# Splitting five heads' outputs at the store instead of at the load, in layer 1 of a two-layer decoder trunk

## The chip, the cores and the metric

The kernel runs on one core of a Trainium2 chip. Its time is the device time of one execution in microseconds (us); the time before is the median of three runs, 1315.35 us (1311.99 to 1317.4). The engines are named as in the profile: PE (TensorE; PEld is its weight loading), DVE (VectorE), ACT (ScalarE), POOL (GpSimd) and SP (SyncE, which here issues nearly all transfers). TensorE's granted clock is given as a share of full speed; 1.00 and 0.50 are its two levels, 2.4 and 1.2 GHz.

## The reference

The input x is one sequence of 1024 positions by 1024 features in fp32. Layer 0 is a differential attention with 6 heads, layer 1 a stick-breaking attention with 12 heads of 64 features on keys and values computed once after layer 0. Both layers also attend to 256 memory tokens with 4 heads, multiply all outputs by a SiLU gate, and end in an output projection whose result is added to the residual. What concerns us is the end of layer 1:

```python
z = einsum(q, k) * scale;  log_beta = log_sigmoid(z)
log_1m = where(mask, log_sigmoid(-z), 0)
suffix = cumsum(log_1m, reverse=True) - log_1m
a = exp(where(mask, log_beta + suffix, -inf));  o = einsum(a, v)
y = concatenate([o, memory_attention]) * silu(gate)      # 1024 x 1024
out = x1 + y @ b_w_out
```

Everything is fp32.

## The kernel before, in words

Every matrix product is made of fp32r operands split in two parts, a "hi" part (a cast to fp32r) and a "lo" part (the value minus that cast). `mm3` (L402) issues three matmuls: hi by hi, hi by lo, lo by hi. So each operand costs a cast and a subtract before PE can use it.

The columns of y are in 8 tiles of 128: tiles 0 to 5 are the heads of layer 1 (each tile holds two of the reference's 12 heads; "head" means such a pair from here on, counted from 0), tiles 6 and 7 are the memory attention. The positions are in two halves c of 512, each of two quarters of 256.

Layer 1 runs in slots (`run_layer`, from n = 0): the memory units take the first 8, and head h takes slots 8 + 8h to 8 + 8h + 8, with its last sums in the slot after. In a slot PE makes scores (`sc`), ACT turns them to sigmoids `u` and `be` (L936, L937), POOL masks `be` (L941), DVE scans `u` (L943) and multiplies `be` by it: that is the weight matrix of one block. One slot later PE transposes it (`tw`, L517; ACT casts it to `wT`, L521, and DVE subtracts), and PE multiplies it with the values (`av`, L965); ACT copies half of that to `avt` (L975), DVE adds it to `y`, POOL multiplies `y` by the gate. The PSUM tiles `tw` and `av` share a pool of three banks, so that a new `tw` may have to wait until DVE's `y` has read an older `av`. `T_`, `ws`, `sc`, `avs` in `run_layer` are these steps' instruction lists, and `merge` interleaves them with the slot's fill work (projections, loads of weights) by cost. This hand-written order is the order of PE's instructions; a scheduler orders those of the other engines, and every engine and queue then works strictly in its own order.

Where does y go? For the last head (h = 5) it goes to `split_y` (L568): ACT casts it into the hi part of `yh`, POOL subtracts for the lo part, both at once in SBUF. The other five heads and the memory tiles go to `store_y` (L543): SP writes the fp32 `y` to `y_dr` in DRAM, since `yh` (pool `hp`, two buffers) takes the place of the hidden state `h`, which is in use until then. `out_proj` (L1005) later loads a tile back (`load`, L1009): a transfer to `ys`, an ACT cast (L1014) and a DVE subtract (L1015), giving `yh` hi and lo. Fourteen such loads are made, seven for each c. Which slot a load goes to is written in `tail` (L1335): B = 48 is the first slot of head 5, `load0` and `load1` are the loads for c = 0 and 1 in the tile order 0, 1, 2, 3, 4, 6, 7, and `go0`, `go1` the products `po` of the output projection.

`ys`, the output weights `w` (raw weights in `raw`, cast at L124, subtract on POOL through the helper at L94), the residual `res` and the memory's `hm` are in one pool, `wp`, with 11 buffers. `L94` is the line of a helper for all tensor-by-tensor operations, so that the tile names tell them apart.

Of the kernel before, what the change touches and what calls it, by code (L numbers as in the profile page):

```python
# [8 lines left out]
F32 = mybir.dt.float32  # L9
F32R = mybir.dt.float32r  # L10
BF16 = mybir.dt.bfloat16
AF = mybir.ActivationFunctionType
ALU = mybir.AluOpType
# [7 lines left out]
NH = 6  # L21
# [18 lines left out]
def trunk(ctx: ExitStack, tc: tile.TileContext, xT, memT, pos, gains, vecs, wA, wAm, wAg, wAo,  # L40
          wB, wBm, wBg, wBo, wM, invf, out):
    nc = tc.nc
    P = 128
# [16 lines left out]
    ppj = ctx.enter_context(tc.tile_pool(name="ppj", bufs=2, space=PSUM))  # L60
    ptr = ctx.enter_context(tc.tile_pool(name="ptr", bufs=3, space=PSUM))

    y_dr = [drp.tile([2, 8, P, 512], F32, name=f"y_dr{l}") for l in range(2)]
    v_dr = [[drp.tile([P, 4, 256], F32, name=f"v_dr{h}{c}") for c in range(2)] for h in range(NH)]
    x1_dr = drp.tile([2, P, 8, 512], F32, name="x1_dr")

# [26 lines left out]
    def tt(eng, out_, a, b, op):  # L93
        eng.tensor_tensor(out_, a, b, op)  # L94
# [303 lines left out]
    def merge(main, fill):  # L398
        for _, f in mixed(main, fill):
            f()  # L400
# [140 lines left out]
        return [(109 * min(4, b + 1 - 4 * g), lambda g=g: go(g)) for g in range((b + 4) // 4)]  # L541

    def store_y(l, t, c, y):  # L543
        nc.sync.dma_start(y_dr[l][c // 2, t, :, (c % 2) * 256:(c % 2) * 256 + 256], y)

    splits = {}

    def y_split(l, c):

        if (l, c) not in splits:  # L550
            splits[(l, c)] = hp.tile([P, 2, 8, 512], F32R, name="yh", tag="h")
        return splits[(l, c)]
# [334 lines left out]
    class StickUnit:  # L887
# [62 lines left out]
        def W(self, bc):  # L950
            b, c = bc
            cc = b // 2
            r = causal_wT(self, b, bc)
            if b % 2 == 0:
                return r, [], []

            def av(part, k0, k1):
                if c == 0 and k0 == 0 and part == 0:
                    self.avt = wk.tile([P, 256], F32, name="avt", tag="tmp")
                if k0 == 0 and part == 0:  # L960
                    self.avp = ptr.tile([P, 512], F32, name="av", tag="tr")
                o = self.avp[:, :256]
                for kb in range(k0, k1):
                    v = self.v[kb // 4][:, kb % 4, 2 * c:2 * c + 2, :]
                    T.matmul(o, v, self.wT[kb // 4][:, part, kb % 4, :], start=(part == 0 and kb == 0),  # L965
                             stop=(part == 1 and kb == b))
                if part == 0 or k1 <= b:
                    return
                if c == 0:
                    self.y = wk.tile([P, 256], F32, name="y", tag="y")  # L970
                tmp = self.avt
                lo, hi = (slice(0, 64), slice(64, 128))
                d, s_ = (lo, hi) if c == 0 else (hi, lo)
                with urgent():
                    S.copy(tmp[d, :], o[s_, :])  # L975
                    tt(V, self.y[d, :], o[d, :], tmp[d, :], ALU.add)
                if c == 1:
                    tt(G, self.y, self.y, silu_cols(1, self.h, cc), ALU.mult)
                    (split_y if self.h == NH - 1 else store_y)(1, self.h, cc, self.y)
            return r, [(218, lambda p=p, k=k: av(p, k, k + 2)) for p in range(2) for k in range(0, b + 1, 2)], []  # L980

    def value_chunks(p, ws, b):
# [22 lines left out]
    def out_proj(l, c, wo):  # L1005
        st = {}
        x1_st[c] = st

        def load(t):  # L1009
            yh = y_split(l, c)  # L1010
            if l == 1:
                ys = wp.tile([P, 512], F32, name="ys", tag="w")
                nc.sync.dma_start(ys, y_dr[l][c, t])
                S.copy(yh[:, 0, t, :], ys)  # L1014
                tt(V, yh[:, 1, t, :], ys, yh[:, 0, t, :].bitcast(F32), ALU.subtract)  # L1015
                return
            ys = vp.tile([P, 2, 512], F32, name="ys", tag="v")
            nc.sync.dma_start(ys, y_dr[l][c, t:t + 2].rearrange("t p n -> p t n"))
            for j in range(2):
                G.tensor_scalar(yh[:, 0, t + j, :], ys[:, j, :], 1.0, 0.0, ALU.mult, ALU.add)  # L1020
                tt(G, yh[:, 1, t + j, :], ys[:, j, :], yh[:, 0, t + j, :].bitcast(F32), ALU.subtract)


        order = tuple(range(8)) if l == 0 else (0, 1, 2, 3, 4, 6, 7, 5)

        def go(m, i):
            if i == 0:
                st["f", m] = load_packed(wo[m], way="act" if m < 2 or (l == 1 and c == 0) else "vector")
                st["ps", m] = ppj.tile([P, 512], F32, name="po", tag="pj")
                if l == 1:  # L1030
                    st["res", m] = wp.tile([P, 512], F32, name="res", tag="w")
                    nc.sync.dma_start(st["res", m], x1_dr[c][:, m, :])
                elif m % 2 == 0:
                    st["res"] = vp.tile([P, 2, 512], F32, name="res", tag="v")
                    nc.sync.dma_start(st["res"], xT[c][:, m:m + 2, :])
            f, yh, ps = st["f", m], y_split(l, c), st["ps", m]
            t = order[i]
            mm3(ps, (f(0, t), f(1, t)), (yh[:, 0, t, :], yh[:, 1, t, :]), i == 0, i == 7)
            if i == 7:
                res = st["res"][:, m % 2, :] if l == 0 else st["res", m]  # L1040
                tt(V, res, ps, res, ALU.add)
                if l == 0:
                    if m == 0:
                        st["a"] = kp.tile([P, 2, 512], F32, name="accs", tag="k")
                    with urgent(HP if m == 7 else 0):
                        squares(st["a"], res, m)
                    if m % 2:
                        nc.sync.dma_start(x1_dr[c, :, m - 1:m + 1, :], st["res"])
                else:
                    nc.sync.dma_start(out[c, m], res)  # L1050
        def without(m, i):

            if i == 0:
                st["f", m] = load_packed(wo[m], way="act")
                st["ps", m] = ppj.tile([P, 512], F32, name="po", tag="pj")
                st["res", m] = wp.tile([P, 512], F32, name="res", tag="w")
                nc.sync.dma_start(st["res", m], x1_dr[c][:, m, :])
            f, yh, ps, t = st["f", m], y_split(l, c), st["ps", m], order[i]
            mm3(ps, (f(0, t), f(1, t)), (yh[:, 0, t, :], yh[:, 1, t, :]), i == 0, i == 6)
            if i == 6:  # L1060
                tt(V, st["res", m], ps, st["res", m], ALU.add)
                if m == EARLY - 1:
                    st["w5"] = load_w(wo[0:EARLY, :, order[7], :].rearrange("m p n -> p m n"), EARLY * P, way="act")

        def last(m):
            yh, w, t = y_split(l, c), st["w5"], order[7]
            ps = ppj.tile([P, 512], F32, name="po", tag="pj")
            o = slice(m * P, (m + 1) * P)
            mm3(ps, (w[:, 0, o], w[:, 1, o]), (yh[:, 0, t, :], yh[:, 1, t, :]), True, True)
            tt(V, st["res", m], ps, st["res", m], ALU.add)  # L1070
            nc.sync.dma_start(out[c, m], st["res", m])
        items = [[(C512, lambda m=m, i=i: go(m, i)) for i in range(8)] for m in range(8)]
        if l == 1 and c == 0:
            items[:EARLY] = [[(C512, lambda m=m, i=i: without(m, i)) for i in range(7)] for m in range(EARLY)]
            items[EARLY + 1:EARLY + 1] = [[(C512, lambda m=m: last(m)) for m in range(EARLY)]]
        return ([(0, lambda t=t: load(t)) for t in ((0, 2, 4) if l == 0 else order[:7])],
                [x for m in items for x in m])

# [193 lines left out]
    def run_layer(l, mem, planned, early, tail):  # L1272
# [4 lines left out]
        for n in range(min(fills), max(ss) + lag + (2 if l == 0 else 1)):  # L1277
# [11 lines left out]
            if l == 0:  # L1289
                sc = flat(sc)  # L1290
                ws, avs = flat(ws), flat(avs)
                if n >= 48:
                    main += fins[:1] + ws + sc[:2] + avs + fins[1:] + sc[2:] + T_
                else:
                    main += fins[:1] + ws + T_ + sc[:2] + avs + fins[1:] + sc[2:]
            else:
                if n > 8:
                    slack = [[(1500, lambda: None)]] if avs else []
                    order = [T_] + ws[:1] + sc[:1] + ws[1:2] + sc[1:2] + slack + avs + sc[2:] + ws[2:]
                else:  # L1300
                    order = ws + sc + [T_] + avs
                main += flat(order)
# [11 lines left out]
    def ends(l, wo):  # L1314
# [17 lines left out]
    load0, go0 = out_proj(1, 0, wBo)  # L1332
    load1, go1 = out_proj(1, 1, wBo)
    B = 8 * NH
    tail = {B + 1: load0[:2], B + 2: load0[2:4] + go0[:4], B + 3: load0[4:] + go0[4:10], B + 4: go0[10:16],  # L1335
            B + 5: go0[16:21], B + 6: go0[21:29], B + 7: go0[29:39], B + 8: go0[39:49] + load1[:2], B + 9: go0[49:55] + load1[2:5]}
    run_layer(1, mems[1], (fills, ts, ss), {}, tail)
    merge([], load1[5:] + go0[55:] + go1)


def _layout(inputs):
# [64 lines left out]
```

## Time and profile before

| | |
|---|---|
| median of three runs | 1315.35 us |
| profiled execution | 1313.52 us |
| its span, first to last instruction | 1311.7 us |
| mean granted clock | 0.98 |
| PE busy | 1241.6 us, 95% of the span |
| PE weight loading | 1107.8 us, 84% |
| DVE busy | 963.2 us, 73% |
| ACT busy | 851.2 us, 65% |
| POOL busy | 729.4 us, 56% |
| chain that ended last | PE 71%, DVE 11%, ACT 5%, DMA 5%, issue 4%, POOL 4% |

The times of the rows below are counted from the first instruction of the span. The shares are averages over the whole span; layer 1's heads run from about 800 us on, head 4 begins near 1082, head 5 near 1155, and the last matmul of the output projection ends near 1308. A wait is the idle time of an engine in front of one instruction, with the instruction that released it. A busy PE at half the clock counts as busy as one at full clock, so stalls and clock have to be read apart.

### The profile page before, as it was taken

How to read it: one execution, taken by the hardware profiler on the slowest of the kernel's cores; microseconds unless marked ns; L12 is line 12 of the kernel's file. 1: busy time of each engine (PE TensorE's matmuls, PEld its weight loads, DVE VectorE, ACT ScalarE, POOL GpSimd, SP SyncE). 2: the span in 40 equal slices, each digit the busy share in tenths (PEclk: the TensorE clock that was granted, in tenths of full speed). 3: DMA queues.
4: the chain of work that ended last, by engine and by line, in shares of the span. 5: the costliest groups of instructions: out<-in, count | busy, mean ns of one | idle time of the engine just before them, and what ended most of it. 6: DMA issues, size and time to landing. Idle time of an engine off the chain costs nothing.

```text
span 1311.7 us, 22804 instructions
## 1 busy us (share of the span) xinstructions
PE 1241.6 (95%) x7396; PEld 1107.8 (84%) x7396; DVE 963.2 (73%) x2129; ACT 851.2 (65%) x2295; POOL 729.4 (56%) x943
## 2 busy tenths in 40 slices
PE   7799999999999899999989999999999999989898
PEld 6699999999999889877868897889788987878777
DVE  8887777788787875864946545897878787788932
ACT  4676667566676766863657866676767676666621
POOL 7664545445353567946046855765666566557620
PEclk9899999999999999999999999999999999989989
DMA  6010101101020222256550142112121222222453
GB/s 220 25 51 27 55 23 43 39 11 60 21 65 21 81 67 77 86 179 222 174 171 25 43 134 61 50 53 92 55 69 35 99 69 64 63 78 91 152 163 114
DMA packets 76071, 105.85 MB, mean 81 GB/s; under 512 B 8368, under 2 KB 60720, under 8 KB 75696
## 3 DMA queue, kind: packets, MB, share of 16 engines
q1 hardware_dynamic: 75664, 104.24, 25.1%
q8 instruction: 59, 0.97, 0.3%
q14 instruction: 60, 0.49, 0.1%
q10 hardware_dynamic: 288, 0.15, 0.0%
HBM read 82.87 MB, written 21.50 MB: 80 GB/s over the span
## 4 chain that ended last, share of the span: by engine, by line
PE 71%; DVE 11%; ACT 5%; DMA 5%; issue 4%; POOL 4%; SPq 0%; DVEq 0%; POOLq 0%; ACTq 0%
PE pq L404 6%; PE pq L406 6%; PE pq L405 6%; PE tw L517 5%; PE pg L404 4%; PE pg L405 4%; PE pg L406 4%; PE sc L506 4%; PE sc L507 3%; PE av L965 3%; PE po L405 2%; PE po L404 2%; PE po L406 2%; PE pv L404 2%; PE pk L404 2%
## 5 line engine op out<-in xcount | busy, mean ns | idle before, releaser
L94 POOL TENSOR_TENSOR w<-raw,w 128x384 fp32r<-128x384 f32 (+1 forms) x183 | 207.0, 1140 | 37.9 <-ACT w L124 30.0
L943 DVE TENSOR_TENSOR_SCAN u<-u,stick 128x128 f32<-128x128 f32 (+3 forms) x96 | 145.2, 1512 | 27.1 <-ACT u L936 26.8
L404 PE MATMUL pq<-w,h 128*128 128x384 f32 (+1 forms) x448 | 159.3, 356 | 6.1 <-ACT h L224 5.5
L94 DVE TENSOR_TENSOR wT<-tw,wT 128x512 fp32r<-128x512 f32 (+2 forms) x248 | 138.6, 565 | 26.0 <-ACT wT L521 24.1
L406 PE MATMUL pq<-w,h 128*128 128x384 f32 (+1 forms) x448 | 148.7, 332 | 3.0 <-DVE h L225 2.9
L405 PE MATMUL pq<-w,h 128*128 128x384 f32 (+1 forms) x448 | 148.3, 331 | 0.8 <-POOL w L94 0.7
L521 ACT CAST wT<-tw 128x512 fp32r<-128x512 f32 (+2 forms) x248 | 121.9, 497 | 33.8 <-PE tw L517 30.7
L941 POOL TENSOR_SCALAR_AFFINE_SELECT be<-be 128x128 f32<-128x128 f32 x96 | 82.2, 857 | 84.8 <-ACT be L937 84.6
L124 ACT CAST w<-raw 128x384 fp32r<-128x384 f32 (+1 forms) x145 | 67.7, 486 | 69.0 <-PE po L406 42.9
L101 POOL TENSOR_TENSOR ss<-ss,mhalf 128x4 f32<-128x4 f32 x68 | 71.2, 1049 | 73.0 <-DVE ss L352 72.3
L404 PE MATMUL pg<-h,w 128*128 128x512 f32 x256 | 109.2, 427 | 0.0
L811 ACT ACTIVATE e<-sc,nmd 128x512 f32<-128x512 f32 (+2 forms) x144 | 82.6, 579 | 36.1 <-DVE nmd L808 33.6
L404 PE MATMUL po<-yh,w 128*128 128x512 f32 x256 | 104.7, 409 | 1.0 <-DVE res L94 0.7
L405 PE MATMUL po<-yh,w 128*128 128x512 f32 x256 | 101.5, 397 | 2.4 <-POOL yh L94 2.4
L405 PE MATMUL pg<-h,w 128*128 128x512 f32 x256 | 103.2, 403 | 0.0
L406 PE MATMUL pg<-h,w 128*128 128x512 f32 x256 | 103.2, 403 | 0.0
L406 PE MATMUL po<-yh,w 128*128 128x512 f32 x256 | 101.3, 396 | 0.0
L517 PE MATMUL tw<-identR,be 128*128 128x128 f32 x432 | 74.7, 284 | 23.0 <-DVE y L94 20.4
L94 DVE TENSOR_TENSOR be<-be,u 128x127 f32<-128x127 f32 (+3 forms) x96 | 83.9, 875 | 14.2 <-POOL be L941 10.3
L404 PEld LDWEIGHTS pq<-w,h 128*128 128x128 f32 x448 | 85.2, 190 | 9.0 <-POOL w L122 5.5
L405 PEld LDWEIGHTS pq<-w,h 128*128 128x128 f32 x448 | 85.4, 191 | 4.0 <-POOL w L94 1.5
L406 PEld LDWEIGHTS pq<-w,h 128*128 128x128 f32 x448 | 84.9, 189 | 4.0 <-DVE h L225 4.0
(239 smaller groups left out, 3914.5 us busy)
## 6 DMA issues: line engine op xcount, KB each, us to landing
raw<-in_wA_dram SPq DMA_DIRECT2D x44, 192.0 KB, 2.4
raw<-in_wBo_dram SPq DMA_DIRECT2D x33, 192.0 KB, 2.5
raw<-in_wAo_dram SPq DMA_DIRECT2D x32, 192.0 KB, 2.8
v_dr<-vs SPq DMA_DIRECT2D x48, 128.0 KB, 1.8
v<-v_dr SPq DMA_DIRECT2D x12, 512.0 KB, 3.4
raw<-in_wB_dram SPq DMA_DIRECT2D x36, 128.0 KB, 2.2
raw<-in_wB_dram SPq DMA_DIRECT2D x24, 192.0 KB, 2.4
wkv<-in_wM_dram SPq DMA_DIRECT2D x16, 256.0 KB, 3.3
```

The costliest lines, as they stand in the source:

```text
L94: eng.tensor_tensor(out_, a, b, op)
L101: G.tensor_tensor(t, t, mhalf[:, :n], ALU.pow)
L124: S.copy(w[:, 0, :n], raw[:, :n])
L404: T.matmul(o, a[0], b[0], start=first, stop=False)
L405: T.matmul(o, a[0], b[1], start=False, stop=False)
L406: T.matmul(o, a[1], b[0], start=False, stop=last)
L506: T.matmul(sc[:, :m], qh, k[:, c, :m], start=True, stop=False)
L517: T.transpose(t[:, j * P:(j + 1) * P], w[:, j * P:(j + 1) * P], identF)
L521: S.copy(hi, t3)
L811: S.activation(e[:, o:o + n], st["sc"][j], AF.Exp, bias=nm[:, 0:1], scale=-1.0 if j == len(ps) - 1 else 1.0, accum_out=st["l"][:, j, c:c + 1])
L941: G.affine_select(out=be[:, L - P:L], in_=be[:, L - P:L], pattern=[[-1, P]], compare_op=ALU.is_gt, fill=0.0, base=0, channel_multiplier=1)
L943: V.tensor_tensor_scan(u[:, 0:L][:, ::-1], u[:, 0:L][:, ::-1], keep["m"][:, 1024 - L:1024][:, ::-1], 1.0, ALU.mult, ALU.max)
```

## The change

`y_dr` gets one more dimension of 2 (hi and lo). For heads 0 to 4 `store_y` is replaced by `store_split`: it only puts a function on the list `late`. `flush`, a step of its own in every slot above 8 behind the first scores, takes what is on the list. In the slot after the sums it makes the split (ACT copies `y` to `ysp` hi, 128x256, POOL subtracts for lo; the buffer is one of `wp`) and puts the store on the list; one slot later it issues the store, 256 KB instead of 128 KB. `load` for tiles 0 to 4 of layer 1 is now one transfer of 512 KB from `y_dr` straight into `yh`, with no cast and no subtract; tiles 6 and 7 are loaded as before. The lists in `tail` move: tiles 6 and 7 of c = 0 to slot B + 2, tile 4 to B + 3, the five of c = 1 from B + 8 and B + 9 to B + 6, and those of tiles 6 and 7 of c = 1 behind two more products at the end.

In numbers: ten of the fourteen casts (128x512, ACT) and ten of the fourteen subtracts (128x512, DVE) go. Twenty ACT copies and twenty POOL subtracts of 128x256 come. Twenty stores and ten loads double in size. PE's instructions and their order are the same.

```diff
--- before.py
+++ after.py
@@ -60,7 +60,7 @@
     ppj = ctx.enter_context(tc.tile_pool(name="ppj", bufs=2, space=PSUM))
     ptr = ctx.enter_context(tc.tile_pool(name="ptr", bufs=3, space=PSUM))
 
-    y_dr = [drp.tile([2, 8, P, 512], F32, name=f"y_dr{l}") for l in range(2)]
+    y_dr = [drp.tile([2, 8, 2, P, 512], F32, name=f"y_dr{l}") for l in range(2)]
     v_dr = [[drp.tile([P, 4, 256], F32, name=f"v_dr{h}{c}") for c in range(2)] for h in range(NH)]
     x1_dr = drp.tile([2, P, 8, 512], F32, name="x1_dr")
 
@@ -541,7 +541,23 @@
         return [(109 * min(4, b + 1 - 4 * g), lambda g=g: go(g)) for g in range((b + 4) // 4)]
 
     def store_y(l, t, c, y):
-        nc.sync.dma_start(y_dr[l][c // 2, t, :, (c % 2) * 256:(c % 2) * 256 + 256], y)
+        nc.sync.dma_start(y_dr[l][c // 2, t, 0, :, (c % 2) * 256:(c % 2) * 256 + 256], y)
+
+    late = []
+
+    def store_split(l, t, c, y):
+
+        def split():
+            s = wp.tile([P, 2, 256], F32R, name="ysp", tag="w")
+            S.copy(s[:, 0, :], y)
+            tt(G, s[:, 1, :], y, s[:, 0, :].bitcast(F32), ALU.subtract)
+            late.append(lambda: nc.sync.dma_start(
+                y_dr[l][c // 2, t, :, :, (c % 2) * 256:(c % 2) * 256 + 256].rearrange("s p n -> p s n"), s.bitcast(F32)))
+        late.append(split)
+
+    def flush():
+        for f in [late.pop(0) for _ in range(len(late))]:
+            f()
 
     splits = {}
 
@@ -976,7 +992,7 @@
                     tt(V, self.y[d, :], o[d, :], tmp[d, :], ALU.add)
                 if c == 1:
                     tt(G, self.y, self.y, silu_cols(1, self.h, cc), ALU.mult)
-                    (split_y if self.h == NH - 1 else store_y)(1, self.h, cc, self.y)
+                    (split_y if self.h == NH - 1 else store_split)(1, self.h, cc, self.y)
             return r, [(218, lambda p=p, k=k: av(p, k, k + 2)) for p in range(2) for k in range(0, b + 1, 2)], []
 
     def value_chunks(p, ws, b):
@@ -1008,14 +1024,17 @@
 
         def load(t):
             yh = y_split(l, c)
+            if l == 1 and t < NH:
+                nc.sync.dma_start(yh[:, :, t, :].bitcast(F32), y_dr[l][c, t].rearrange("s p n -> p s n"))
+                return
             if l == 1:
                 ys = wp.tile([P, 512], F32, name="ys", tag="w")
-                nc.sync.dma_start(ys, y_dr[l][c, t])
+                nc.sync.dma_start(ys, y_dr[l][c, t, 0])
                 S.copy(yh[:, 0, t, :], ys)
                 tt(V, yh[:, 1, t, :], ys, yh[:, 0, t, :].bitcast(F32), ALU.subtract)
                 return
             ys = vp.tile([P, 2, 512], F32, name="ys", tag="v")
-            nc.sync.dma_start(ys, y_dr[l][c, t:t + 2].rearrange("t p n -> p t n"))
+            nc.sync.dma_start(ys, y_dr[l][c, t:t + 2, 0].rearrange("t p n -> p t n"))
             for j in range(2):
                 G.tensor_scalar(yh[:, 0, t + j, :], ys[:, j, :], 1.0, 0.0, ALU.mult, ALU.add)
                 tt(G, yh[:, 1, t + j, :], ys[:, j, :], yh[:, 0, t + j, :].bitcast(F32), ALU.subtract)
@@ -1296,7 +1315,7 @@
             else:
                 if n > 8:
                     slack = [[(1500, lambda: None)]] if avs else []
-                    order = [T_] + ws[:1] + sc[:1] + ws[1:2] + sc[1:2] + slack + avs + sc[2:] + ws[2:]
+                    order = [T_] + ws[:1] + sc[:1] + [[(0, flush)]] + ws[1:2] + sc[1:2] + slack + avs + sc[2:] + ws[2:]
                 else:
                     order = ws + sc + [T_] + avs
                 main += flat(order)
@@ -1332,10 +1351,10 @@
     load0, go0 = out_proj(1, 0, wBo)
     load1, go1 = out_proj(1, 1, wBo)
     B = 8 * NH
-    tail = {B + 1: load0[:2], B + 2: load0[2:4] + go0[:4], B + 3: load0[4:] + go0[4:10], B + 4: go0[10:16],
-            B + 5: go0[16:21], B + 6: go0[21:29], B + 7: go0[29:39], B + 8: go0[39:49] + load1[:2], B + 9: go0[49:55] + load1[2:5]}
+    tail = {B + 1: load0[:4], B + 2: go0[:2] + load0[5:6] + go0[2:4] + load0[6:], B + 3: load0[4:5] + go0[4:10], B + 4: go0[10:16],
+            B + 5: go0[16:21], B + 6: load1[:5] + go0[21:29], B + 7: go0[29:39], B + 8: go0[39:49], B + 9: go0[49:55]}
     run_layer(1, mems[1], (fills, ts, ss), {}, tail)
-    merge([], load1[5:] + go0[55:] + go1)
+    merge([], go0[55:57] + load1[5:] + go0[57:] + go1)
 
 
 def _layout(inputs):
```

At the start of head 5 DVE has this order in the kernel before, from the cast keys `k` of head 5 to the `y` of head 4 that frees the bank for the next transposes (`u<-u,stick` is the scan, `tw` and `wT` the transposed weights):

```order
L94 TENSOR_TENSOR k<-pk,k 64x512 x2
L94 TENSOR_TENSOR yh<-ys,yh 128x512 x4
L94 TENSOR_TENSOR wT<-tw,wT 128x3x128
L943 SCALAR_TENSOR_TENSOR u<-u,stick 128x896
...
L943 SCALAR_TENSOR_TENSOR u<-u,stick 128x1024
L94 TENSOR_TENSOR yh<-ys,yh 128x512
L94 TENSOR_TENSOR be<-be,u 128x1023
L94 TENSOR_TENSOR yh<-ys,yh 128x512
L94 TENSOR_TENSOR ql<-pq,qh 64x512 x2
L94 TENSOR_TENSOR yh<-ys,yh 128x512
L94 TENSOR_TENSOR y<-av,avt 64x256
```

The same place in the kernel after (its lines are 16 higher):

```order
L94 TENSOR_TENSOR k<-pk,k 64x512 x2
L94 TENSOR_TENSOR wT<-tw,wT 128x3x128
L959 SCALAR_TENSOR_TENSOR u<-u,stick 128x896
L94 TENSOR_TENSOR wT<-tw,wT 128x4x128
L94 TENSOR_TENSOR be<-be,u 128x895
L94 TENSOR_TENSOR wT<-tw,wT 128x4x128
L959 SCALAR_TENSOR_TENSOR u<-u,stick 128x1024
L94 TENSOR_TENSOR be<-be,u 128x1023
L94 TENSOR_TENSOR ql<-pq,qh 64x512 x2
L94 TENSOR_TENSOR y<-av,avt 64x256
```

The seven subtracts of `yh` that stood between `k` and `y` are gone from the place.

At the start of head 4 ACT has this order in the kernel before, from the `avt` of head 3 through the two pieces of sigmoids of a block of seven tiles (L152 casts turned weights):

```order
L975 COPY avt<-av 64x256
L521 CAST wT<-tw 128x4x128
L914 CAST k<-pk 64x512 x2
L521 CAST wT<-tw 128x3x128
L936 ACTIVATE u<-sc 128x512
L937 ACTIVATE be<-sc 128x512
L936 ACTIVATE u<-sc 128x384
L937 ACTIVATE be<-sc 128x384
```

And in the kernel after:

```order
L991 COPY avt<-av 64x256
L521 CAST wT<-tw 128x4x128
L930 CAST k<-pk 64x512 x2
L521 CAST wT<-tw 128x3x128
L552 CAST ysp<-y 128x256
L152 ACTIVATE w<-raw,gn 128x128 x3
L952 ACTIVATE u<-sc 128x512
L953 ACTIVATE be<-sc 128x512
L952 ACTIVATE u<-sc 128x384
L953 ACTIVATE be<-sc 128x384
```

The copy of the `y` of head 3 has come between `wT` and the sigmoids, and with it three casts of weights that stood behind them.

In the last slot DVE has this order before, from a scan to the last head's `y`:

```order
L943 SCALAR_TENSOR_TENSOR u<-u,stick 128x1024
L94 TENSOR_TENSOR yh<-ys,yh 128x512
L94 TENSOR_TENSOR res<-po,res 128x512
L94 TENSOR_TENSOR yh<-ys,yh 128x512
L94 TENSOR_TENSOR be<-be,u 128x1023
L94 TENSOR_TENSOR yh<-ys,yh 128x512
L94 TENSOR_TENSOR y<-av,avt 64x256
```

And after:

```order
L959 SCALAR_TENSOR_TENSOR u<-u,stick 128x1024
L94 TENSOR_TENSOR be<-be,u 128x1023
L94 TENSOR_TENSOR res<-po,res 128x512
L94 TENSOR_TENSOR yh<-ys,yh 128x512 x2
L94 TENSOR_TENSOR y<-av,avt 64x256
```

Only the subtracts of tiles 6 and 7 are left, and both stand directly ahead of `y`.

## Rows read from the trace of the kernel before

**Rows 1.** The page, part 1: busy us, share of the span, instructions.
```profile
PE 1241.6 (95%) x7396; PEld 1107.8 (84%) x7396; DVE 963.2 (73%) x2129; ACT 851.2 (65%) x2295; POOL 729.4 (56%) x943
```

**Rows 2.** Waits of PE, then SP's queue: line, releaser: us in total, times, longest.
```profile
PE tw L517 <- DVE y L94: 20.4, 7, 6.8
...
SPq L544 <- POOL y L94: 100.0, 22, 15.1
```

**Rows 3.** PE's timeline: start us, us, instruction, [idle before <-releaser].
```profile
675.30 1.02 PE L233 MATMUL ms<-onesD,accs 128*128 128x1 f32 x8 [2.13 <-DVE accs L94]
...
947.09 0.66 PE L517 MATMUL tw<-identR,be 128*128 128x128 f32 x4 [2.86 <-DVE y L94]
...
1094.85 1.11 PE L517 MATMUL tw<-identR,be 128*128 128x128 f32 x4 [2.90 <-DVE y L94]
...
1172.89 1.11 PE L517 MATMUL tw<-identR,be 128*128 128x128 f32 x4 [5.71 <-DVE y L94]
...
1248.99 1.11 PE L517 MATMUL tw<-identR,be 128*128 128x128 f32 x4 [6.85 <-DVE y L94]
```

**Rows 4.** Stretches: engines' busy us (instructions), granted clock, DMA share, GB/s.
```profile
675.00:679.00 4.00, 3.70 (x31) 3.73 (x32) 0.95 (x5) 1.36 (x4) 4.00 (x5) 1.00 0.60 211
...
1170.00:1176.00 6.00, 3.11 (x12) 2.71 (x13) 5.14 (x10) 1.50 (x3) 1.92 (x4) 0.50 0.45 130
...
1245.00:1255.00 10.00, 6.01 (x19) 5.04 (x20) 6.38 (x8) 2.88 (x6) 4.71 (x5) 0.50 0.61 184
1260.00:1300.00 40.00, 40.00 (x179) 33.10 (x178) 12.99 (x25) 9.38 (x20) 2.27 (x3) 1.00 0.55 172
```

**Rows 5.** DVE's timeline, start of head 5: one y to the next.
```profile
1154.14 0.43 DVE L94 TENSOR_TENSOR y<-av,avt 64x256 f32<-64x256 f32 x1
...
1172.42 0.42 DVE L94 TENSOR_TENSOR y<-av,avt 64x256 f32<-64x256 f32 x1
```

**Rows 6.** DVE's groups of instructions, 1154 to 1173: busy us, mean ns, idle before.
```profile
L94 DVE TENSOR_TENSOR yh<-ys,yh 128x512 fp32r<-128x512 f32 x7 | 5.7, 849 | 0.1
```

**Rows 7.** Tile yh, from 1100 on: ns min/median/max, first and last start.
```profile
L404 PE MATMUL po<-yh,w x128: 389/389/775, 1182.6 to 1307.0; 128*128 128x512 f32 x128
...
L1014 ACT CAST yh<-ys x14: 614/622/717, 1155.6 to 1241.4; 128x512 fp32r<-128x512 f32 x14
L94 DVE TENSOR_TENSOR yh<-ys,yh x14: 676/710/1479, 1157.0 to 1247.1; 128x512 fp32r<-128x512 f32 x14
L571 ACT CAST yh<-y x4: 403/406/410, 1195.0 to 1259.9; 128x256 fp32r<-128x256 f32 x4
L94 POOL TENSOR_TENSOR yh<-y,yh x4: 738/841/1062, 1196.6 to 1260.8; 128x256 fp32r<-128x256 f32 x4
```

**Rows 8.** ACT's timeline, head 4's last sums.
```profile
1179.92 0.36 ACT L975 COPY avt<-av 64x256 f32<-64x256 f32 x1 [2.60 <-PE av L965]
```

**Rows 9.** Timelines of ACT, POOL and DVE at the start of head 4.
```profile
1080.79 0.60 ACT L936 ACTIVATE u<-sc 128x512 f32<-128x512 f32 x1
...
1086.31 0.99 ACT L152 ACTIVATE w<-raw,gn 128x128 fp32r<-128x128 f32 x3 [0.18 <-PE pq L406]
...
1081.55 0.73 POOL L94 TENSOR_TENSOR y<-y,sl 128x256 f32<-128x256 f32 x1 [3.42 <-DVE y L94]
...
1089.09 2.87 POOL L94 TENSOR_TENSOR w<-raw,w 128x384 fp32r<-128x384 f32 x1
...
1084.11 2.16 DVE L943 TENSOR_TENSOR_SCAN u<-u,stick 128x896 f32<-128x896 f32 x1
...
1088.37 2.79 DVE L943 TENSOR_TENSOR_SCAN u<-u,stick 128x1024 f32<-128x1024 f32 x1
```

**Rows 10.** DVE's timeline in the last slot.
```profile
1240.52 2.28 DVE L943 TENSOR_TENSOR_SCAN u<-u,stick 128x1024 f32<-128x1024 f32 x1
...
1248.52 0.41 DVE L94 TENSOR_TENSOR y<-av,avt 64x256 f32<-64x256 f32 x1
```

**Rows 11.** Tile ys: from issue to landing.
```profile
DMA to landing us min/median/max: 2.5/3.1/4.8
```

## The prediction

> **What bounds the kernel now.** I read the page's busy shares first, then the waits of TensorE, then where on TensorE's timeline those waits lie, and last what the releasing engine did before each. PE is busy for 1241.6 of 1311.7 us [rows 1]: whatever leaves PE's own order alone can win only PE's idle time, and time in which PE runs below full clock. The change leaves PE's instructions and their order as they are. Of PE's waits in layer 1 one kind is large, the transpose of new weights into tw, released by VectorE's y: 20.4 us in 7 waits [rows 2]. Four of them make 18.3 us: 2.86 and 2.90 at the starts of heads 2 and 4 (counted from 0), 5.71 at the start of head 5 and 6.85 in the last slot [rows 3]. I call the last two A and B. tw doesn't read y; it takes the PSUM bank that y is last to read.
>
> The clock is the second price. After A it stands at 0.50 in 1170 to 1176, after B in 1245 to 1255 [rows 4], the lower of its two levels. PE resumed at 1172.89 and ran about 3.5 us at half rate, so lost 1.75; after B it resumed at 1248.99 and ran 5.9 us so (to about 1255), and lost 3.0. A pause of 2.13 us at 675.30 left the clock at 1.00 [rows 3, 4]; after the 2.90 one at 1094.85 four transposes took 1.11 us, as after A and B, at the half rate [rows 3]. So the price of the clock falls away only where a pause is cut to about 2 us. From 1260 to 1300 PE is busy for 40.00 of 40.00 us at 1.00 [rows 4]: nothing can be won there.
>
> **A: the start of head 5.** VectorE goes from one y at 1154.14 to the next at 1172.42 with hardly a gap [rows 5], and seven subtracts yh<-ys,yh take 5.7 us of that [rows 6]. The new order has none of them there; five of the ten removed ones belong to this place, and the other two go later, with their tiles. y would then start near 1166.8 and end near 1167.2. PE is ready at 1172.89 - 5.71 = 1167.18 and needs a moment after y. I take a remaining wait of 0.4, which also covers ACT's later avt, so 5.3 us of stall and all 1.75 of clock: -7.0. That the transfers now write yh in place puts nothing late: all five wait for the hidden state's last product, as the casts did, and the first product from yh is at 1182.6 [rows 7].
>
> **First weights of the output projection.** In the new order POOL has the ysp subtract of head 4's last columns ahead of the first three subtracts of weights, and ACT its copy ahead of their casts. The chain is avt at 1179.92 [rows 8], y, POOL's product with the gate, ACT's copy at 0.41, a cast, then POOL's 0.84 for ysp [rows 7] and one subtract for w. With about 0.5 us for each small step it ends near 1183.9, 1.3 after the first product's present start. Bounds: 0 if the weights' subtract slips ahead of that chain's end, 4 if POOL's instructions stretch as in [rows 9] (2.87 for one). I take +1.3.
>
> **B: the last slot.** Here five direct loads replace five load, cast and subtract triples, and only tiles 6 and 7 keep the old form. VectorE's scan at 1240.52 waits today for ACT's u, which stand behind casts, and behind it come subtracts, be and only at 1248.52 y [rows 10]. Without the five tiles' casts and subtracts, scan and be are done near 1242. What is late next is the load of tiles 6 and 7. Its buffer is freed by PE's last use of an older weight, by PE's order some 3.9 us of work ahead of the waiting tw, which is due at 1248.99 - 6.85 = 1242.14: so issue near 1238.25. With 3.1 us to landing [rows 11], two casts and the last subtract (0.62, 0.71 [rows 7]), and y, tw goes at about 1244.2: a wait of 2.1 in place of 6.85, -4.75. That is just where the clock's price is decided; I take half of its 3.0. B: -6.2. Bounds: -8.2 (transfer at its fastest, clock kept) and -3.2 (a wait of 3.7, clock lost).
>
> **Starts of heads 2 and 4.** Here the change costs. ACT's new copy of y stands ahead of the sigmoids u and be of the slot, and waits for POOL. In the trace the first u runs at 1080.79, while POOL's y starts at 1081.55 and takes 0.73 [rows 9], so ends at 1082.28. ACT stands for 1.4 us, copies for 0.41, and the order puts three casts of weights, 0.99 together [rows 9], ahead of u too. u comes about 2.8 us later. Its four sigmoids end near 1082.6 today and VectorE, busy with k and wT, starts the 896 scan at 1084.11 [rows 9]: 1.4 us of cover. So y comes about 1.4 later at each place: +2.8. Bounds: -4.6, if the scans run at the 2.28 of [rows 10] and not at 2.79 [rows 9], and +5.8, the whole 2.9 twice. At heads 1, 3 and 5 the y of POOL is done when ACT comes to the copy, and I count 0.
>
> One row on VectorE and POOL together bears on this: the scan of 128x1024 takes 2.79 us at 1088.37, where POOL's subtract of w runs beside it from 1089.09 for 2.87, and 2.28 at 1240.52 [rows 9, 10]. The Trainium skill (SBUF — State Buffer, section "SBUF: two separate sides") says that VectorE and GpSimd share one port pair as an exclusive lock, which a VectorE instruction with two SBUF inputs and a GpSimd one that reads SBUF can't hold together. The trace agrees in sign: both are longer. By that rule the change moves ten 128x512 subtracts off VectorE but adds twenty to POOL, and one lands beside a scan or a be at heads 2 and 4: 0.84 each, +1.7 in all, and the sum would be 1309 rather than 1307.
>
> **The other stores.** Of 20 stores, those outside head starts fall where PE has work queued. An ACT copy of 0.41 and a POOL subtract of 0.84 [rows 7] go in, 8.1 and 16.8 us in all, on engines 65% and 56% busy [rows 1]. SP already waits for y at 22 stores for 100.0 us [rows 2]; the store now waits for ysp one slot later, and behind it stand the same loads of weights. The transfers double, 128 KB to 256 KB; the ones from y_dr land in 2.5 to 4.8 us today [rows 11], and a slot is several times that. Zero is the lower bound, 4 the upper (0.2 at each); I take +1.5, since one or two of them find ACT just ahead of POOL as at head 4.
>
> **The sum.** -7.0 + 1.3 - 6.2 + 2.8 + 1.5 = -7.6. The profiled execution took 1313.52 us, its span 1311.7 and 1.8 around it, so 1305.9. The median shown is 1315.35, 1.8 above that run; from it the sum gives 1307.7. I forecast 1307, between them.
>
> **Rivals.**
> First, ACT's copy delays every slot (slower). ACT works in order, so each of the 20 copies can hold the u and be behind it, and with them scan, be and y. For it: the 1.4 us that ACT stands at head 4's start, where u today runs before y is done [rows 9]. Against it: PE waits for y in only 7 places [rows 2], so most slots have cover. Price: 1.3 us at each of 20 is +26, against -13.2 from A and B and +1.3 for the first weights: 1313.5 + 14 = 1328. It decides from an average of 0.6 us per store ((13.2 - 1.3)/20), and makes the kernel slower.
> Second, the gain at B turns into a wait for the load of tiles 6 and 7. ACT runs the two casts ahead of avt, so a late load also holds avt, y and tw. For it: today ys lands in 2.5 to 4.8 us [rows 11] and SP has a queue of weight loads. Then B gives 3.2 and the first weights cost 4: -7.0 + 4 - 3.2 + 2.8 + 1.5 = -1.9, 1312 to 1313: no change that counts.
> Third, the added work is hidden anyway: B gives its 8.2, head starts and stores cost nothing, weights arrive in time: -15.2, 1298 to 1300. For it: ACT and POOL have a third and more of the time free; against it the queue order at head 4.
> That the change doesn't do what it says gets no chance: the new instruction order holds the copies and lacks the subtracts.
>
> **How the numbers follow.** Forecast 45% (own range 1302 to 1311), ACT's copies 12%, load at B 23%, all hidden 20%. A measurement of this kernel tells 0.5%, 6.6 us, from no change: below 1308.8 is faster, above 1321.9 slower. Four fifths of the forecast and all of the third rival are faster, 0.56; the rest of the forecast and nearly all of the second, 0.32; 0.12 slower. The range, 1297 to 1319, leaves out the first rival and the best part of the third.
>
> **What would show it.** A: in the new profile the wait for y at the start of head 5 under 1 us and no 0.50 clock there. B: a wait of about 2 us, with the load of ys landing just before it. Heads 2 and 4: waits of 4 to 4.5 us in place of 2.9, and ACT idle before the ysp copy with POOL's y as releaser. First weights: PE idle about 1 us before po, released by POOL. I'm wrong if tw waits for y grow in slots where today there are none, or if B keeps over 3.5 us.

## The result, and the profile after

The changed kernel takes 1320.49 us (median of 20 runs, 1314.15 to 1326.28), the kernel before 1313.63 in the same runs (1306.97 to 1317.87): a ratio of 1.0051, 95% interval 1.0039 to 1.0063. It is slower by half a per cent, where 1307 was forecast. The profiled execution has a span of 1319.5 us, 7.8 longer than before. PE's busy time is the same (1241.6 before), so the difference is in its idle time; what the clock costs or gives back is inside the busy time and has to be counted apart.

The page's busy line of the kernel after, and below it PE's waits (us in total, times, longest); they stand against [rows 1, 2]:

```profile
PE 1241.5 (94%) x7396; PEld 1108.0 (84%) x7396; DVE 964.8 (73%) x2119; ACT 852.4 (65%) x2305; POOL 735.0 (56%) x963
```

```profile
PE tw L517 <- DVE y L94: 12.6, 6, 3.7
PE tw L517 <- DVE be L94: 10.4, 5, 2.6
...
PE pv L404 <- DVE k L94: 4.4, 2, 2.2
```

The waits for y have fallen from 20.4 to 12.6 us. Two kinds are there that the rows of before don't show as large ones: tw that waits for be, and the value products pv that wait for k (pv takes the PSUM bank that k is read from). PE's timeline after, from layer 1's heads on (start us, us, instruction, idle before; most waits under 1 us are left out):

```profile
831.54 0.63 PE L517 MATMUL tw<-identR,be 128*128 128x128 f32 x4 [1.98 <-DVE be L94]
...
876.29 0.66 PE L517 MATMUL tw<-identR,be 128*128 128x128 f32 x4 [1.49 <-DVE y L94]
...
890.13 0.35 PE L404 MATMUL pv<-wf,h 128*128 128x256 f32 x1 [2.18 <-DVE k L94]
...
953.91 1.11 PE L517 MATMUL tw<-identR,be 128*128 128x128 f32 x4 [3.65 <-DVE y L94]
...
985.38 0.63 PE L517 MATMUL tw<-identR,be 128*128 128x128 f32 x4 [2.44 <-DVE be L94]
...
1030.13 0.66 PE L517 MATMUL tw<-identR,be 128*128 128x128 f32 x4 [1.48 <-DVE y L94]
...
1044.00 0.36 PE L404 MATMUL pv<-wf,h 128*128 128x256 f32 x1 [2.18 <-DVE k L94]
...
1109.32 0.66 PE L517 MATMUL tw<-identR,be 128*128 128x128 f32 x4 [3.65 <-DVE y L94]
...
1140.99 1.01 PE L517 MATMUL tw<-identR,be 128*128 128x128 f32 x4 [2.50 <-DVE be L94]
...
1186.31 0.66 PE L517 MATMUL tw<-identR,be 128*128 128x128 f32 x4 [0.49 <-DVE y L94]
...
1195.72 0.50 PE L406 MATMUL po<-yh,w 128*128 128x512 f32 x1 [0.74 <-POOL w L94]
...
1220.67 0.75 PE L981 MATMUL av<-wT,v 128*128 128x256 f32 x4 [2.00 <-DVE wT L94]
...
1259.46 0.66 PE L517 MATMUL tw<-identR,be 128*128 128x128 f32 x4 [1.84 <-DVE y L94]
```

Against [rows 3]: A, the start of head 5, waits 0.49 and no longer 5.71; B, the last slot, 1.84 and no longer 6.85. The starts of heads 2 and 4 wait 3.65 instead of 2.86 and 2.90, those of heads 1 and 3 wait 1.49 and 1.48 instead of 0.56 and 0.52. And five waits are new, all where one head's work is well under way: 1.98, 2.44 and 2.50 in heads 0, 2 and 4, and 2.18 twice, in heads 1 and 3; 11.3 us together.

The clock in four stretches after, two with a new wait, then A and B:

```profile
1040.00:1060.00 20.00, 17.82 (x133) 17.34 (x131) 15.24 (x25) 11.75 (x34) 12.17 (x18) 0.91 0.26 85
1140.00:1160.00 20.00, 19.00 (x97) 16.26 (x98) 15.23 (x20) 9.09 (x21) 6.63 (x8) 0.91 0.08 24
1180.00:1200.00 20.00, 18.71 (x112) 15.75 (x110) 16.14 (x26) 12.29 (x31) 8.74 (x15) 1.00 0.54 170
1240.00:1260.00 20.00, 18.16 (x108) 15.60 (x107) 18.07 (x19) 11.29 (x25) 12.82 (x13) 1.00 0.44 134
```

A and B now run at 1.00 [rows 4 has 0.50 there]; two of the new waits lose 0.09 of 20 us each, 1.8.

What makes the new waits? First head 4 at 1140.99. DVE's row of the scan that be and so tw wait for, then what POOL did from 1132 on:

```profile
1134.67 4.87 DVE L959 TENSOR_TENSOR_SCAN u<-u,stick 128x512 f32<-128x512 f32 x1
```

The same scan in the kernel before:

```profile
1118.56 1.21 DVE L943 TENSOR_TENSOR_SCAN u<-u,stick 128x512 f32<-128x512 f32 x1
```

And POOL after:

```profile
1132.22 0.73 POOL L94 TENSOR_TENSOR ysp<-y,ysp 128x256 fp32r<-128x256 f32 x1
...
1134.08 1.61 POOL L94 TENSOR_TENSOR raw<-raw,gn 128x384 f32<-128x384 f32 x2
1135.65 1.00 POOL L94 TENSOR_TENSOR w<-raw,w 128x384 fp32r<-128x384 f32 x1
1136.62 0.28 POOL L957 TENSOR_SCALAR_AFFINE_SELECT be<-be 128x128 f32<-128x128 f32 x1
1136.88 1.01 POOL L94 TENSOR_TENSOR w<-raw,w 128x384 fp32r<-128x384 f32 x1
1137.85 0.61 POOL L94 TENSOR_TENSOR raw<-raw,gn 128x256 f32<-128x256 f32 x1
...
1138.67 1.39 POOL L94 TENSOR_TENSOR w<-raw,w 128x256 fp32r<-128x256 f32 x1
```

While the scan's row lasts, from 1134.67 to 1139.54, POOL works off weights without a gap; the last of three products ends at 1138.46, the scan 1.1 us later, and the subtract that POOL starts at 1138.67 ends only after the scan. Such a scan of 128x512 with 4.83 to 4.88 us stands in heads 0, 2 and 4, and nowhere else in the kernel. POOL's run begins when ACT has cast the weights, and ACT's timeline in head 4 and in head 3 shows when that is:

```profile
1131.38 0.41 ACT L552 CAST ysp<-y 128x256 fp32r<-128x256 f32 x1 [0.32 <-POOL y L94]
1131.70 1.86 ACT L152 ACTIVATE w<-raw,gn 128x128 fp32r<-128x128 f32 x6
```

```profile
1037.19 0.43 ACT L552 CAST ysp<-y 128x256 fp32r<-128x256 f32 x1
1037.51 1.87 ACT L152 ACTIVATE w<-raw,gn 128x128 fp32r<-128x128 f32 x6
1039.28 0.36 ACT L952 ACTIVATE u<-sc 128x256 f32<-128x256 f32 x1
1039.54 0.37 ACT L953 ACTIVATE be<-sc 128x256 f32<-128x256 f32 x1
1039.81 0.69 ACT L152 ACTIVATE w<-raw,gn 128x128 fp32r<-128x128 f32 x2
1040.39 1.16 ACT L930 CAST k<-pk 64x512 fp32r<-64x512 f32 x2
```

Each time six of the eight casts of one weight stand in a row right behind the copy ysp, and the other two soon after. In head 3 they stand ahead of u for 1.9 us and ahead of k for another 0.7; DVE's half of k follows late, and pv waits 2.18 for it. In the kernel before the same eight casts are spread over the slots, three, three and two in head 3, and three and five in head 4, with u, be and k between them:

```profile
1109.80 0.98 ACT L152 ACTIVATE w<-raw,gn 128x128 fp32r<-128x128 f32 x3
...
1111.90 1.17 ACT L914 CAST k<-pk 64x512 fp32r<-64x512 f32 x2
1113.10 1.58 ACT L152 ACTIVATE w<-raw,gn 128x128 fp32r<-128x128 f32 x5
```

### The profile page after: what moved, and what is told of

The parts are those of the page before. It is cut to its first block, busy times and chain, and to the rows that moved or that the text cites. A ratio compares the mean times of both kernels' runs of the same rounds, so it can differ in the third digit from the quotient of the medians.

```text
span 1319.5 us, 22731 instructions
## 1 busy us (share of the span) xinstructions
PE 1241.5 (94%) x7396; PEld 1108.0 (84%) x7396; DVE 964.8 (73%) x2119; ACT 852.4 (65%) x2305; POOL 735.0 (56%) x963
## 4 chain that ended last, share of the span: by engine, by line
PE 62%; DVE 14%; POOL 8%; ACT 6%; issue 6%; DMA 4%; SPq 0%; POOLq 0%; DVEq 0%; ACTq 0%
PE pq L404 6%; PE pq L406 6%; PE pq L405 6%; PE tw L517 5%; PE sc L506 3%; PE pg L404 3%; PE pg L405 3%; PE pg L406 3%; PE sc L507 3%; PE av L981 3%; PE po L404 3%; PE po L405 3%; PE po L406 3%; DVE u L959 2%; PE pv L404 2%
## 5 line engine op out<-in xcount | busy, mean ns | idle before, releaser
L94 POOL TENSOR_TENSOR w<-raw,w 128x384 fp32r<-128x384 f32 (+1 forms) x183 | 194.3, 1071 | 27.1 <-ACT w L124 17.3
L959 DVE TENSOR_TENSOR_SCAN u<-u,stick 128x128 f32<-128x128 f32 (+3 forms) x96 | 150.9, 1572 | 37.3 <-ACT u L952 37.1
L957 POOL TENSOR_SCALAR_AFFINE_SELECT be<-be 128x128 f32<-128x128 f32 x96 | 88.4, 922 | 100.6 <-ACT be L953 96.9
L94 DVE TENSOR_TENSOR be<-be,u 128x127 f32<-128x127 f32 (+3 forms) x96 | 87.5, 914 | 14.6 <-POOL be L957 10.2
L517 PE MATMUL tw<-identR,be 128*128 128x128 f32 x432 | 73.1, 279 | 23.1 <-DVE y L94 12.6
```

The lines of the kernel that those rows point to most:

```text
L517: T.transpose(t[:, j * P:(j + 1) * P], w[:, j * P:(j + 1) * P], identF)
L957: G.affine_select(out=be[:, L - P:L], in_=be[:, L - P:L], pattern=[[-1, P]], compare_op=ALU.is_gt, fill=0.0, base=0, channel_multiplier=1)
L959: V.tensor_tensor_scan(u[:, 0:L][:, ::-1], u[:, 0:L][:, ::-1], keep["m"][:, 1024 - L:1024][:, ::-1], 1.0, ALU.mult, ALU.max)
```

## The experiments

Why do the casts line up behind ysp? **Theory W**: `ysp` is one of the 11 buffers of `wp`, the pool of the weights, and buffers are given out in the order of the program text. A weight that stands behind ysp in the text gets no buffer until ysp, which waits for y, has had its turn. **Rival Q**: the buffers don't matter; ACT in its own order simply stands for POOL's y, and everything behind it is late. **Theory T** is on the other side of the account: A and B gain by the direct loads, and the loss is the split's.

**Only the lists of loads.**

```diff
--- before
-    tail = {B + 1: load0[:2], B + 2: load0[2:4] + go0[:4], ...
+    tail = {B + 1: load0[:4], B + 2: go0[:2] + load0[5:6] + ...     # the changed kernel's lists
```

> The kernel before with only the new lists of loads (no split at the store, tiles still loaded, cast and subtracted). Theory T (the gain of the change comes from the direct loads at A and B, its loss from the split): A keeps its five subtracts of tiles 0 to 4, so the wait at the start of head 5 stays at 4 to 6 us; B has its five loads earlier, so it falls from 6.9 to about 2 us with the clock kept: 1305 to 1308. Rival R (only the removed casts and subtracts help): B's work moves into slots that have none free, and the time stays at 1313 or grows.

Measured: 1311.10 us, ratio 0.9979 (0.9959 to 0.9998), above the 1305 to 1308 of T and below the 1313 of R. PE's timeline of this kernel, A, a new wait and B:

```profile
1174.11 1.12 PE L517 MATMUL tw<-identR,be 128*128 128x128 f32 x4 [5.71 <-DVE y L94]
...
1204.91 0.63 PE L517 MATMUL tw<-identR,be 128*128 128x128 f32 x4 [2.09 <-ACT be L937]
...
1249.07 0.65 PE L517 MATMUL tw<-identR,be 128*128 128x128 f32 x4 [1.79 <-DVE y L94]
```

A stays and B goes, as T says. But some slots earlier, where the five triples of load, cast and subtract now stand, are waits of 2.09 and 1.00 us (the kernel before has one of 1.02 there), and the clock falls to 0.91 in 1200 to 1220. So B's gain needs no direct load, only earlier loads; A's does. The own-buffers kernel below, with direct loads, has neither of these two waits.

**ysp in buffers of its own.**

```diff
-            s = wp.tile([P, 2, 256], F32R, name="ysp", tag="w")
-            S.copy(s[:, 0, :], y)
+            hi = wk.tile([P, 256], F32R, name="ysp", tag="sq")
+            lo = wk.tile([P, 256], F32R, name="ysp", tag="A")
+            S.copy(hi, y)
...
-            late.append(lambda: nc.sync.dma_start(...))      # one store, 256 KB
+            late.append(go)                                  # two stores, 128 KB each
```

> The changed kernel with ysp in two tiles of other tags (hi in that of sq, lo in that of A) instead of a buffer of the weights' pool, so two stores of 128 KB in place of one of 256 KB. Theory W (ysp takes its turn among the weights' buffers, so that casts of weights line up behind the copy of y, and POOL then works them off in one burst): the three scans of 128x512 that took 4.87 us go back to 1.2, the waits of 2.0 to 2.5 us at heads 0 to 4 go, and the time falls to 1303 to 1308. Rival Q (ACT in its order stands for POOL's y, whichever buffer it writes): 1319 to 1324, waits as in the changed kernel.

Measured: 1305.89 us, ratio 0.9920 (0.9894 to 0.9946). The scan at the same place:

```profile
1116.99 1.21 DVE L963 TENSOR_TENSOR_SCAN u<-u,stick 128x512 f32<-128x512 f32 x1
```

The waits of 2.18 for k are down to 0.62, no scan of 128x512 is long, and the starts of heads 2 and 4 wait 2.36 and 1.93. A is back at 2.51, and two scans of 128x640 take 3.6 us (3.1 in the kernel before). The same copies and subtracts with other buffers are 14.6 us faster than the changed kernel by the medians. ACT's order shows the turn itself (the numbers are those of the buffers' requests in the order of the program text). In head 2, first the changed kernel, then the one with own buffers:

```
L552 CAST ysp_12477<-y_12358 128x256 [waits Pool_49]
L152 ACTIVATE w_12531<-raw_12529,gn_139 128x128 [waits DMAHW3_49]

L152 ACTIVATE w_12548<-raw_12546,gn_139 128x128 [waits DMAHW2_49,PE_49]
...
L553 CAST ysp_12493<-y_12373 128x256 [waits DMAHW0_49,Pool_49]
```

In the changed kernel no w with a higher number comes before ysp, at any of the 20 copies; with own buffers w 12548 comes well ahead of ysp 12493, and some w with a higher number ahead of 14 of the 20. Q has fallen: ACT still waits for POOL's y there. Two things are not told apart by any run: the order of the turns, and that the weights have a buffer less while ysp is in use. And with the buffers one store became two smaller ones.

**The copy on POOL.**

```diff
-            S.copy(s[:, 0, :], y)
+            G.tensor_scalar(s[:, 0, :], y, 1.0, 0.0, ALU.mult, ALU.add)
```

> The changed kernel with the hi copy made by POOL, not by ACT; the buffers stay in the weights' pool. Rival Q (ACT stands for POOL's y): the waits at the starts of heads 2 and 4 fall from 3.65 to 2.9 and below, time 1308 to 1314. Theory W (turn among the weights' buffers): casts of weights still stand behind ysp, the long scans stay or grow with POOL's 20 copies of about 0.6 us: 1320 to 1328.

Measured: 1325.19 us, ratio 1.0070 (1.0044 to 1.0095). ACT has nothing to stand for, and the time grows; the three long scans take 5.47 to 5.49 us, the head starts 3.52. This is W's number and the opposite of Q's.

**The split beside the old loads**, in the weights' pool and then in own buffers. The old store, loads and lists stay; ysp and its store go to a part of `y_dr` that nothing reads.

```diff
     def store_split(l, t, c, y):
+        store_y(l, t, c, y)
...
-    tail = {B + 1: load0[:4], ...          # and load() as in the kernel before
+    tail = {B + 1: load0[:2], ...
```

> The kernel before, with its lists and its loads, and the split and its store beside (as in the changed kernel, to a part of y_dr that nothing reads). It shows the cost of the split alone. If the gain at A and B was 15 us in the changed kernel, as its trace has it, and the rest cost 22: 1333 to 1338. If the split is cheap and the lists cost: 1314 to 1318.

> As the split-beside kernel (lists and loads of before, the split and its store beside), but ysp in the tiles of the other tags. Theory W: of the 17 us that the split cost beside in the weights' pool, 12 or more go: 1315 to 1320. Rival Q (the split itself costs): 1328 to 1333.

Measured: in the weights' pool 1330.97 us, ratio 1.0114 (1.0084 to 1.0144), a little under the 1333 to 1338 expected; in own buffers 1314.40, ratio 1.0005 (0.9988 to 1.0021), even less than W's 1315 to 1320. B and one of the new waits of the first, then A and B of the second:

```profile
988.75 0.63 PE L517 MATMUL tw<-identR,be 128*128 128x128 f32 x4 [2.52 <-DVE be L94]
...
1268.24 1.12 PE L517 MATMUL tw<-identR,be 128*128 128x128 f32 x4 [6.85 <-DVE y L94]
```

```profile
1174.86 1.11 PE L517 MATMUL tw<-identR,be 128*128 128x128 f32 x4 [5.70 <-DVE y L94]
...
1251.03 1.12 PE L517 MATMUL tw<-identR,be 128*128 128x128 f32 x4 [6.84 <-DVE y L94]
```

(In the first, A waits 1.42 only: its subtracts stand later there, and po waits up to 1.01 for yh.) Twenty ACT copies, twenty POOL subtracts and their stores cost nothing that can be measured. The pool that the copy takes its buffer from costs 16.6 us by the medians (1330.97 against 1314.40), 14.3 by the ratios.

**The split one slot later still**, in own buffers.

```diff
-        late.append(split)
+        late.append(lambda: late.append(split))
```

> As the own-buffers kernel, and the split is made one slot later still, so that y is done long before ACT comes to it. If ACT standing for POOL's y costs what is left at the starts of heads 2, 4 and 5 (2.36, 1.93 and 2.51 us there): waits fall by 1 us each, 1302 to 1305. If it is only the two more instructions per store: 1305 to 1307, as the own-buffers kernel.

Measured: 1306.21 us, ratio 0.9941 (0.9924 to 0.9957), the same as the own-buffers kernel. ACT's standing for y is worth nothing more; the waits left at the starts of heads 2, 4 and 5 (2.38, 2.37, 2.51) are released by VectorE's y, and what holds that up wasn't followed further.

**All tiles split at the store**, in own buffers, the memory's too (its slots get a `flush` for it).

```diff
-            store_y(l, t, c, y)
+            store_split(l, t, c, y)
...
-            if l == 1 and t < NH:
+            if l == 1:
```

> As the own-buffers kernel, and tiles 6 and 7 (the memory attention) are split at the store too, so that no load of layer 1 needs a cast or a subtract. The last wait of the own-buffers kernel in the last slot, 1.76 us, should fall under 0.5: 1303 to 1305 against its 1306. If the eight more splits among the first slots cost as much: 1306 to 1308.

Measured: 1313.25 us, ratio 0.9990 (0.9972 to 1.0007), where 1303 to 1308 was expected. B's wait falls to 0.96, not under 0.5, and the profile has this in the memory's slots, on PE and on ACT:

```profile
761.84 0.55 PE L404 MATMUL pv<-wf,h 128*128 128x256 f32 x1 [6.38 <-DVE vs L94]
...
761.10 0.43 ACT L1017 CAST vs<-pv 128x128 fp32r<-128x128 f32 x2 [1.50 <-DMA y_dr<-ysp]
```

The value tiles vs use the tags sq and A, just those that ysp was moved to, and ACT's cast of vs waits for the store of ysp. It is a wait for a buffer once more: ysp now takes turns with vs.

**How a scan and POOL share.** Three sets of small trials measure the long scan by itself.

```diff
+    def subs(n):
+        for i in range(n):
+            G.tensor_tensor(wr[:, i, :].bitcast(F32R), raw, gate[:, :384], ALU.subtract)
...
+            S.copy(gate, last)
+            S.copy(u, src)
...
+                pool(n)
+            dve(u)
```

> Not the trunk: only small trials, three of each, its output has no meaning. ACT writes a tile that starts n POOL subtracts of 128x384 (n = 0, 1, 2, 4, 8), and 0.6 us later a tile that starts one scan of 128x512 on VectorE; then a VectorE multiply of two SBUF tiles and a VectorE subtract with one PSUM operand beside 4 POOL subtracts, and a scan beside 4 POOL scalings with one tile operand. Theory P (a VectorE instruction with two SBUF operands gets no turn while POOL works on back to back): the scan's row grows with n, from 1.2 us to about 2, 3, 4 to 5 and 8 to 9. Rival S (each waits for the other's instruction at most once): the row stays under 2.5 us for every n, and POOL's subtracts are the ones that stretch. The PSUM form stays at 0.69 under both.

> Again small trials, three of each, no trunk. In the first trials VectorE and POOL always fell in step the same way; here POOL's run starts 0.1 to 0.6 us ahead of VectorE's instruction (a, b, c: one scan beside 8 subtracts; d: three scans; e, f: a multiply of two SBUF tiles), and g to j repeat POOL's run of the changed kernel at 1132 to 1140 (subtract, two gain products, subtract, mask, subtract, product, memset, subtract) beside one scan, a PSUM subtract and a scan, three scans. If the scan's 4.87 us in the kernel is VectorE losing several turns in a row to POOL: some of g to j, or of a to f at other offsets, show a scan of 3 us and more. If each loses one turn at most: all scans stay under 2.2 us, and the 4.87 has to come from something that isn't in the trials.

> Small trials, four of each, no trunk. The earlier trials had POOL instructions that don't wait for anything; here POOL's run is made as the kernel makes it: weights by transfer, casts with gains on ACT, POOL's product in place, then its subtract that reads the product, so that each waits on ACT or on POOL itself. a, b, c: with the mask and the memset between, VectorE's scan of 128x512 starting at three offsets; d, e: without them. If it is these chained instructions that take several turns in a row: scans of 3 us and more in a to e, near 4.9 where the offset fits. If not: all under 2.2 us, and the 4.87 us in the kernel stays open.

DVE's rows of the first set: the scan alone, beside one and beside eight subtracts, and the PSUM form alone and beside four; then POOL's eight:

```profile
9.10 1.22 DVE L65 TENSOR_TENSOR_SCAN au<-au,stick 128x512 f32<-128x512 f32 x1 [9.10 <-ACT au L83]
...
16.38 1.62 DVE L65 TENSOR_TENSOR_SCAN bu<-bu,stick 128x512 f32<-128x512 f32 x1 [1.20 <-ACT bu L83]
...
52.31 1.61 DVE L65 TENSOR_TENSOR_SCAN eu<-eu,stick 128x512 f32<-128x512 f32 x1 [3.89 <-ACT eu L83]
...
101.05 0.69 DVE L100 TENSOR_TENSOR hu<-ps,hu 128x512 fp32r<-128x512 f32 x1 [3.95 <-ACT hu L83]
...
106.73 0.69 DVE L100 TENSOR_TENSOR iu<-ps,iu 128x512 fp32r<-128x512 f32 x1 [1.20 <-ACT iu L83]
```

```profile
51.83 8.57 POOL L72 TENSOR_TENSOR wr<-raw,gate 128x384 fp32r<-128x384 f32 x8 [0.73 <-ACT gate L82]
```

A scan that comes during a subtract takes 1.61 us, beside one subtract or eight: it waits for the end of one, and POOL waits for it in turn (four subtracts take 4.78 us beside a scan, 3.86 beside the PSUM form). In the second set the longest single scan took 1.93, in the third, with POOL's run made as in the kernel, 2.07. So theory P, that a scan loses many turns in a row, isn't confirmed; S, that each loses one turn at most, has it in the trials. What makes the scan of the kernel take 4.87 us, as if it lost some four turns, stays open.

## Why the prediction was wrong

- **A** was right. -7.0 was forecast; the wait fell by 5.2 and 1.75 of clock came back.
- **B** was right in its mechanism and sized too low: -6.2, half of the clock's price counted in. The wait fell by 5.0 (2.1 left was forecast, 1.84 is) and the clock's 3.0 came back whole: -8.0. Just ahead of it ACT waits 1.44 us for the load of ys, as the forecast says.
- **First weights**: +1.3 forecast, 0.74 measured, with POOL's w as releaser, as said.
- **Starts of heads 2 and 4**: +2.8 forecast, +1.5 measured. Heads 1 and 3, counted at 0, took +0.9 and +1.0. Together +3.4. The reason given, ACT's standing for y, isn't the one: with the copy on POOL the starts still wait 3.52, and with own buffers, where ACT stands as before, 2.36 and 1.93, less than in the kernel before.
- **The other stores**: this is the step that failed. It priced the copy and the subtract by their own time, 0.41 and 0.84 us, and the waits of ACT for y, took +1.5 with 4 as the upper bound, and put the clock at nothing there. Measured, the term is 17.7: 11.3 us of new waits, 3.6 of clock, and 2.8 more at 1216 to 1225 in the tail's slots (waits of 0.82, 2.00 and 0.96, where 1.02 was before). The forecast's sign of being wrong looked at waits for y alone; the new ones are for be and k. The runs show that the split itself costs nothing that can be measured (1.0005 beside the old loads), and that nearly all of the term goes with the buffer it is given (1.0114 in the weights' pool). What was missed is a resource, not a duration: the new tile was added to a pool whose other users wait in the order of their requests.

The terms of the trace make -7.0 - 8.0 + 0.7 + 3.4 + 11.3 + 3.6 + 2.8 = +6.8, against 7.8 between the spans; about 1 us is lost before layer 1's heads, where the two programs hardly differ. With own buffers the change gives 1305.89, and 1307 was forecast, but that is in part luck, since the terms are others: in that kernel's trace A keeps 2.51, the starts of heads 2 and 4 wait less than before instead of more, and five new waits of 0.62 to 1.25 make 4.5.

The first rival forecast slower, 1328, but its mechanism, ACT standing for POOL's y at each of 20 stores, is not what the runs show: five places carry most of the cost, and it goes with the buffers. A clue was shown with the change: three casts of weights behind ysp at head 4's start. The prediction counted their 0.99 us there and didn't ask why they had moved, nor whether they had elsewhere.

On VectorE and POOL, the trials give the rows that the prediction hadn't: an SBUF scan goes from 1.22 to 1.61 us beside a subtract, a subtract with a PSUM operand stays at 0.69. The Trainium skill (SBUF — State Buffer, section "SBUF: two separate sides") has an exclusive port pair for just such pairs of instructions, held for a whole instruction; the trials agree. The scan of 4.87 us goes beyond one instruction, and no run here says why.

## What to carry to other kernels

When a change takes a buffer from a pool, list who else takes buffers there and what they wait for: a tile that waits for late data can hold up every later request, as ysp did here, however short its own work is. Look at the new order for instructions that the change doesn't name but that have moved, and ask what holds them, at every place where the pattern repeats. An experiment with the same instructions and other buffers tells the price of the work from the price of the buffer in one run.

## What the runs showed of the hardware

A pause of PE doesn't have a fixed price. The kernel before has one more that the prediction didn't use, in layer 0:

```profile
559.83 0.50 PE L405 MATMUL po<-yh,w 128*128 128x512 f32 x1 [2.08 <-POOL yh L94]
```

After it the clock was 0.91 in 560 to 580, while the 2.13 us at 675.30 left it at 1.00. In the changed kernel 2.18 us ahead of pv left 1.00 in 880 to 900 and 0.91 in 1040 to 1060. In the lists-only kernel two pauses of 2.92 and 2.90 us left the clock at 1.00 in the stretches around them, where the kernel before has 0.91 in 1080 to 1100 after 2.90. The own-buffers kernel's profiled execution kept 1.00 through 2.36 and 2.51, the one with the later split lost some of it after 2.38 and 2.51 (0.91 and 0.92 over 20 us). The eight executions of the own-buffers kernel themselves had mean clocks from 0.980 to 0.988 and times from 1299.91 to 1309.42, so one profile of each kernel doesn't tell what a pause costs in it. The point that the prediction put at about 2 us is no sharp line.
